# Two subtractions of the second layer's attention heads moved from the Vector engine to GpSimd

## The chip, the core and the metric

The kernel runs on one core of a Trainium2 chip. A core has five engines that run at the same time, each with its own instruction queue that it works through in order: TensorE (PE in the rows, its weight loads PEld), VectorE (DVE), ScalarE (ACT), GpSimd (POOL) and SyncE (SP), which here issues DMAs. An instruction that waits for a semaphore holds up everything behind it in its own queue, and nothing else. The metric is the device time of one execution in microseconds (us); lower is better.

## The reference, cut to what matters

Two sequences of 528 tokens (16 learned tokens and 512 given ones) go through two layers. The first is a bidirectional gated DeltaNet, the second is multi-head latent attention with 16 heads, each with 128 plain and 64 rotated ("rope") dimensions:

```python
q = (cq @ w_uq).reshape(B, L, MLA_HEADS, MLA_DQK)
kv = (ckv @ w_ukv).reshape(B, L, MLA_HEADS, MLA_NOPE + MLA_DV)
...
q = _rmsnorm(q, qk_q_g)
k = _rmsnorm(k, qk_k_g)
q = jnp.concatenate([q[..., :MLA_NOPE], _rope(q[..., MLA_NOPE:], cos, sin)], axis=-1)
k = jnp.concatenate([k[..., :MLA_NOPE], _rope(k[..., MLA_NOPE:], cos, sin)], axis=-1)
...
s = jnp.einsum('bqhd,bkhd->bhqk', qblk, k, preferred_element_type=jnp.float32) * scale
p = jax.nn.softmax(s, axis=-1)
return jnp.einsum('bhqk,bkhd->bqhd', p.astype(v.dtype), v)
...
y = o.reshape(B, L, MLA_V_WIDTH) * jax.nn.silu(z)
return y @ w_out
```

## The kernel before

Everything is fp32. A product a·b of two fp32 matrices is made of three TensorE passes: each operand is split into a high part (a cast to fp32r, by ScalarE) and a low part (the operand less its high part, a subtraction by `sub`, line 88), and `mm3` (lines 75 to 77) adds high·high, high·low and low·high. So nearly every tile costs one cast on ScalarE and one `sub` on VectorE or GpSimd. Weights are split by `weights`: the cast `wh` on ScalarE (line 219) and the low part `wl` on GpSimd (line 88); `last_wl` remembers the newest of these subtractions. As `sub` is a helper, all its instructions carry line 88, and the tile names tell them apart.

The second layer takes the heads in pairs, 8 for each sequence, 16 in all. While one pair's scores, softmax and outputs run (`pair_scores`, `pair_out`, eight query blocks), the generator `head` prepares the next pair: keys (`pair_k`), the rotated query (`pair_qrope`, whose half swap goes through DMA), its split (`pair_qsplit`), queries (`pair_q`), values (`pair_v`), normed keys (`pair_knorm`) and gates (`pair_z`). The order within an engine is settled when the program is built, by a scheduler with a timing model of its own. `behind` hands it an ordering edge: what is traced inside is queued behind the given instructions on the same engine.

The names that the steps below use:
- `acc` of line 964: the rotated query of both heads, the sum of two products that GpSimd made (lines 956, 957). VectorE adds them.
- `SQ` and `RL`: high and low part of the rotated query. Each is stacked with the other half (`SIDES`), so that one 128-row pass on TensorE does two of the three products. Per pair there are two `RL` subtractions of 64x512, both inputs in SBUF.
- `kst`: the rotated key, high part in one half of the partitions and low part in the other. Per pair two `kst` subtractions of 64x528, both inputs in SBUF.
- `mx`, `sm`, `P`: per block the negated row maximum (line 1089, read from PSUM; scaled in line 1090), the exponentials with their sum (line 1093, ScalarE), its reciprocal (line 1094) and the normed probabilities (line 1096, VectorE). TensorE transposes `P` (lines 1108 and 1110).
- `qL` (line 1012) and `hnL<-pj` (line 88): low parts of the queries and of the values, read by VectorE from the two projection buffers `pj` in PSUM. A buffer is free for the next projection when this has been done.
- `sqr` (line 1014 on GpSimd, then line 1015 on VectorE): sums of squares. The second needs the first.
- `kr` (line 1055): keys times their norm. `hnH<-tr`: low part of the transposed probabilities.

Of the kernel before, what the change touches and what calls it, by code (L numbers as in the profile page):

```python
# [23 lines left out]
class Trunk:  # L24
# [935 lines left out]
    def pair_qsplit(self, u):  # L960
        nc = self.nc
        V, A, G, PE = nc.vector, nc.scalar, nc.gpsimd, nc.tensor
        qg, sw = u["qg"], u["sw"]
        V.tensor_tensor(qg, qg, sw, op=ALU.add)
        RL = self.RL[u["hp"] % 2]
        SQ = [self.t("SQ%d" % j, [128, 512], F32R) for j in range(2)]
        for j, (o, nn) in enumerate(self.SIDES):
            A.copy(SQ[j][o], qg[o])
            nc.sync.dma_start(SQ[j][nn].bitcast(F32), SQ[j][o].bitcast(F32))
            self.sub(V, RL[j][o], qg[o], SQ[j][o])  # L970
        u.update(RL=RL, SQ=SQ)

    def pair_k(self, u):
# [76 lines left out]
    def pair_knorm(self, u, j):  # L1050
        nc = self.nc
        V, A, G, PE = nc.vector, nc.scalar, nc.gpsimd, nc.tensor
        c, kr, rs = u["c"], u["kr"], u["rs"]
        o, nn = self.SIDES[j]
        V.tensor_tensor(kr[:, j], kr[:, j], rs[:, j], op=ALU.mult)
        u["k"][j] = self.split("k", kr[:, j], [128, T])
        kp = self.t("acc", [128, T])
        G.tensor_tensor(kp, c["kpr"], rs[:, j], op=ALU.mult)
        kst = self.t("kst", [128, T], F32R)
        A.copy(kst, kp)  # L1060
        self.sub(V, kst[nn], kp[nn], kst[nn])
        u["kst"][j] = kst

    def pair_z(self, u, j):
# [64 lines left out]
    def run(self, rc, rs):  # L1129
# [76 lines left out]
        def head(u):  # L1206
            self.pair_k(u)
            yield
            self.pair_qrope(u)
            yield  # L1210
            with self.behind(self.last_sc, self.last_P):
                self.pair_qsplit(u)
            if u["hp"]:
                yield
            self.pair_q(u, 0)
            yield
            if u["hp"]:
                self.pair_v(u)
                with self.behind(self.last_sc, self.last_P, self.last_wl):
                    self.pair_knorm(u, 0)  # L1220
                yield
            self.pair_q(u, 1)
            with self.behind(self.last_sc, self.last_P, self.last_wl):
                if not u["hp"]:
                    self.pair_knorm(u, 0)
                self.pair_knorm(u, 1)
            yield
            self.pair_z(u, 0)
            yield
            if u["hp"] == 0:  # L1230
                self.pair_v(u)
                yield
# [13 lines left out]

        ends = [self.out_proj(y2[s], I["mla_w_out"][0], h1[s], hq[s], NM, 512, [tC, tA], finish(s)) for s in range(2)]
        fill = chain(self.l2_prep(0, h1[0], rsd[0], ctx[0]), head(units[0]))
        S = self.p("S", [128, 2, 512])
        pss[1] += [S[:, c, 0:264] for c in range(2)]  # L1250
# [10 lines left out]
        for i, u in enumerate(units):  # L1261
            edge = i % 8 == 7
            if not edge:
                fill = head(units[i + 1])
            else:
                fill = chain(self.l2_prep(1, h1[1], rsd[1], ctx[1]), head(units[8])) if i == 7 else ends[0]
            zat = 0 if i == 15 else 2
            for n in range(8):
                if n == zat and i != 7:
                    self.pair_z(u, 1)  # L1270
                for _ in range((2, 1, 2, 2, 2, 2, 2, 2)[n] if i == 7 else int(n > 0 or not edge)):
                    next(fill, None)
                if i == 6 and n == 7:
                    self.pair_z(units[7], 1)
                S, P = u["SP"]
                if n < 7:
                    self.pair_scores(u, (n + 1) // 4, (n + 1) % 4)
                elif i == 7:
                    drain(fill)
                    self.pair_scores(units[8], 0, 0)  # L1280
                elif i < 15:
                    self.pair_scores(units[i + 1], 0, 0)
                self.pair_out(u, n // 4, n % 4, S, P)
# [48 lines left out]
```

## Time and profile before

| | us |
|---|---|
| median of 3 runs | 2628.21 (2627.2 to 2632.5) |
| the profiled execution | 2632.01 |
| its span from first to last instruction | 2630.3 |

| engine | busy us | share of the span |
|---|---|---|
| TensorE | 2468.7 | 94% |
| VectorE | 1732.9 | 66% |
| ScalarE | 1408.4 | 54% |
| GpSimd | 1166.6 | 44% |

The profiled execution took 2632.01 us, 1.7 us more than its span, and lies 0.14% over the median. TensorE is the engine with the least idle time. The pairs of the second layer run from about 1500 to 2420 us of the span, and the lines that the diff touches run nowhere else. A row of the timeline is: start, duration, engine, line, operation, output and inputs, shapes, count; in brackets the idle time of the engine before it and what ended that wait. A row of a stretch is: the stretch, its length, busy us (and count) of PE, PEld, DVE, ACT and POOL, the granted TensorE clock (PEclk, 1.00 for the level of 2.4 GHz, 0.50 for that of 1.2 GHz), the busy share of the DMA engines, and GB/s.

### The profile page before, as it was taken

To read this page: it belongs to the slowest core of one execution; us is meant where nothing else is said; L and a number is where in the kernel's file an instruction comes from. 1 tells how busy PE (TensorE), PEld (TensorE's weight loads), DVE (VectorE), ACT (ScalarE), POOL (GpSimd) and SP (SyncE) were. 2 spreads that over 40 slices of the span, in tenths; PEclk is the share of its full clock that TensorE was granted. 3 is DMA by queue.
4 is the path that set the end of the run, shared out by engine and by line. 5 is a ranking of instruction groups with operands and counts; after the bars stand their busy time and mean duration, and the time that the engine had idled before them with its cause. 6 is when DMAs were issued, how large, how long until landed. Compare 5 with 4: busy or idle time off the path is not lost.

```text
span 2630.3 us, 52159 instructions
## 1 busy us (share of the span) xinstructions
PE 2468.7 (94%) x19083; PEld 2212.1 (84%) x19083; DVE 1732.9 (66%) x3915; ACT 1408.4 (54%) x3424; POOL 1166.6 (44%) x1157
## 2 busy tenths in 40 slices
PE   8889999998999999999989889998998989999999
PEld 7878888888888889888989878888887878888787
DVE  6987888777788867786454256667775567666421
ACT  5545655545455554545545365666656556665432
POOL 6544545432433323323445454555535544554343
PEclk9999999988999999999999999999999999999999
DMA  6544545442333354444465422233332223225575
GB/s 206 176 121 136 153 128 164 136 138 86 112 91 90 113 172 138 133 122 144 127 213 167 130 79 71 73 72 83 90 89 74 81 70 69 77 69 153 167 222 148
DMA packets 453216, 321.06 MB, mean 122 GB/s; under 512 B 134812, under 2 KB 364430, under 8 KB 452960
## 3 DMA queue, kind: packets, MB, share of 16 engines
q1 hardware_dynamic: 452960, 317.73, 41.9%
q8 instruction: 150, 2.46, 0.4%
q14 instruction: 106, 0.87, 0.1%
HBM read 216.02 MB, written 92.67 MB: 117 GB/s over the span
## 4 chain that ended last, share of the span: by engine, by line
PE 58%; DVE 20%; DMA 8%; ACT 6%; issue 4%; POOL 2%; SPq 2%; ACTq 0%; POOLq 0%; DVEq 0%
PE pj L75 12%; PE pj L76 12%; PE pj L77 12%; PE ch L692 2%; PE po L710 2%; DVE acc L374 2%; DVE RL L88 2%; DMA acc<-acc 2%; DVE Yt L504 1%; DVE kq L374 1%; PE ch L703 1%; DVE Y L506 1%; PE lv L552 1%; PE tr L1110 1%; DMA T<-Td 1%
## 5 line engine op out<-in xcount | busy, mean ns | idle before, releaser
L88 POOL TENSOR_TENSOR wl<-wraw,wh 128x512 fp32r<-128x512 f32 (+2 forms) x414 | 547.6, 1325 | 708.8 <-ACT wh L219 675.3
L75 PE MATMUL pj<-hnH,wh 128*128 128x264 f32 (+4 forms) x2080 | 632.8, 305 | 18.9 <-ACT wh L219 5.2
L77 PE MATMUL pj<-hnH,wl 128*128 128x264 f32 (+3 forms) x2080 | 627.6, 303 | 2.6 <-POOL wl L88 1.9
L76 PE MATMUL pj<-hnL,wh 128*128 128x264 f32 (+3 forms) x2080 | 625.2, 301 | 0.7 <-DVE hnL L784 0.6
L219 ACT CAST wh<-wraw 128x512 fp32r<-128x512 f32 (+2 forms) x414 | 248.2, 600 | 346.0 <-PE pj L76 195.8
L75 PEld LDWEIGHTS pj<-hnH,wh 128*128 128x128 f32 (+1 forms) x2080 | 398.9, 192 | 37.6 <-ACT wh L219 5.7
L77 PEld LDWEIGHTS pj<-hnH,wl 128*128 128x128 f32 (+1 forms) x2080 | 398.3, 192 | 17.8 <-POOL wl L88 3.3
L76 PEld LDWEIGHTS pj<-hnL,wh 128*128 128x128 f32 (+1 forms) x2080 | 399.0, 192 | 15.8 <-issue 2.5
L76 PE MATMUL pj<-h2L,wh 128*128 128x512 f32 (+1 forms) x544 | 205.5, 378 | 3.2 <-DVE h2L L88 3.1
L77 PE MATMUL pj<-h2H,wl 128*128 128x512 f32 (+1 forms) x544 | 205.8, 379 | 0.0
L75 PE MATMUL pj<-h2H,wh 128*128 128x512 f32 (+1 forms) x544 | 205.4, 379 | 0.3
L1089 DVE TENSOR_REDUCE mx<-S 128x1 f32<-128x528 f32 x128 | 89.9, 703 | 66.3 <-PE S L1086 65.5
L1093 ACT ACTIVATE P<-S,mx,qs 128x528 f32<-128x528 f32 x128 | 101.5, 793 | 46.6 <-DVE mx L1090 42.7
L76 PEld LDWEIGHTS pj<-h2L,wh 128*128 128x128 f32 x544 | 102.5, 188 | 22.4 <-DVE h2L L88 4.4
L732 POOL TENSOR_TENSOR oa<-oa,ot 128x256 f32<-128x256 f32 (+1 forms) x80 | 69.6, 870 | 114.5 <-DVE ot L730 101.2
L75 PEld LDWEIGHTS pj<-h2H,wh 128*128 128x128 f32 x544 | 102.3, 189 | 20.0 <-DVE cqL L916 0.6
L77 PEld LDWEIGHTS pj<-h2H,wl 128*128 128x128 f32 x544 | 102.7, 189 | 18.1
L374 DVE SCALAR_TENSOR_TENSOR acc<-raw,vec,acc 128x528 f32<-128x528 f32 x128 | 112.4, 881 | 6.7 <-ACT acc L372 5.7
L374 DVE SCALAR_TENSOR_TENSOR kq<-raw,vec,kq 128x528 f32<-128x528 f32 x128 | 105.7, 826 | 8.6 <-ACT kq L372 7.6
L793 DVE TENSOR_TENSOR raw<-raw,pj 128x512 f32<-128x512 f32 (+1 forms) x54 | 31.3, 580 | 120.9 <-PE pj L77 120.7
L1116 ACT CAST hnH<-tr 128x512 fp32r<-128x512 f32 x128 | 74.9, 585 | 61.5 <-PE tr L1110 59.6
L88 DVE TENSOR_TENSOR hnH<-tr,hnH 128x512 fp32r<-128x512 f32 x128 | 88.2, 689 | 19.6 <-ACT hnH L1116 16.1
(483 smaller groups left out, 6789.1 us busy)
## 6 DMA issues: line engine op xcount, KB each, us to landing
wraw<-in_gdn_w_in_dram SPq DMA_DIRECT2D x96, 256.0 KB
wc<-wh SPq DMA_DIRECT2D x96, 256.0 KB
wc<-wl SPq DMA_DIRECT2D x96, 256.0 KB
wh<-wc SPq DMA_DIRECT2D x96, 256.0 KB
wl<-wc SPq DMA_DIRECT2D x96, 256.0 KB
wraw<-in_mla_w_in_dram SPq DMA_DIRECT2D x88, 256.0 KB
wraw<-in_gdn_w_out_dram SPq DMA_DIRECT2D x64, 256.0 KB
wraw<-in_mla_w_out_dram SPq DMA_DIRECT2D x64, 256.0 KB
```

The costliest lines, as they stand in the source:

```text
L75: mm(out, ah, bh, start=first, stop=False)
L76: mm(out, ah, bl, start=False, stop=False)
L77: mm(out, al, bh, start=False, stop=last)
L88: return eng.tensor_tensor(out, a, hi, op=ALU.subtract)
L219: nc.scalar.copy(wh, raw)
L374: nc.vector.scalar_tensor_tensor(acc, raw[:, j:j + T], self.convw(j, u), acc, op0=ALU.mult, op1=ALU.add)
L692: PE.matmul(pc[:n, 0], kq[:, 0, sl], S[d], start=True, stop=True)
L710: PE.matmul(po[:n, 0], kq[:, 1, sl], S[d], start=True, stop=True)
L732: G.tensor_tensor(oa[:n, i], oa[:n, i], t, op=ALU.add)
L1089: V.tensor_reduce(mx, Sv, axis=AX.XY, op=ALU.max, negate=True)
L1093: self.last_P = A.activation(P, Sv, AF.Exp, bias=mx, scale=qs[j][:, qt:qt + 1], accum_out=sm)
L1116: A.copy(PTH[:, :, hc], pt)
```

## The change

`pair_qsplit` and `pair_knorm` make their subtractions with `G` (GpSimd) in place of `V` (VectorE). The ordering edges for `pair_qsplit` get `last_wl` added, a GpSimd instruction; the split of keys had that edge already. Nothing else is edited.

```diff
@@ pair_qsplit
         for j, (o, nn) in enumerate(self.SIDES):
             A.copy(SQ[j][o], qg[o])
             nc.sync.dma_start(SQ[j][nn].bitcast(F32), SQ[j][o].bitcast(F32))
-            self.sub(V, RL[j][o], qg[o], SQ[j][o])
+            self.sub(G, RL[j][o], qg[o], SQ[j][o])
@@ pair_knorm
         A.copy(kst, kp)
-        self.sub(V, kst[nn], kp[nn], kst[nn])
+        self.sub(G, kst[nn], kp[nn], kst[nn])
@@ run, head
-            with self.behind(self.last_sc, self.last_P):
+            with self.behind(self.last_sc, self.last_P, self.last_wl):
                 self.pair_qsplit(u)
```

The scheduler then orders the second layer anew. VectorE's queue in the third pair, before, from the sum of the rotated query (line 964) to the first normed probabilities behind it (line 1096):

```order
L964 TENSOR_TENSOR acc<-acc 128x512
L1125 SCALAR_TENSOR_TENSOR zs<-x,zs 128x256
L1089 TENSOR_REDUCE mx<-S 128x1
L88 TENSOR_TENSOR RL_19078<-acc,SQ_21907 64x512
L88 TENSOR_TENSOR RL_19079<-acc,SQ_21908 64x512
L1090 TENSOR_SCALAR mx<-mx,qs 128x1
L88 TENSOR_TENSOR hnH<-tr,hnH 128x4x128
L1094 RECIPROCAL sm<-sm 128x1
L1096 TENSOR_SCALAR P<-P,sm 128x528
```

The same stretch of VectorE's queue in the changed kernel:

```order
L964 TENSOR_TENSOR acc<-acc 128x512
L1125 SCALAR_TENSOR_TENSOR zs<-x,zs 128x256
L1089 TENSOR_REDUCE mx<-S 128x1
L1090 TENSOR_SCALAR mx<-mx,qs 128x1
L88 TENSOR_TENSOR hnH<-tr,hnH 128x4x128
L1094 RECIPROCAL sm<-sm 128x1
L1096 TENSOR_SCALAR P<-P,sm 128x528
```

The two RL rows that stood between the row maximum and the probabilities are gone from here, and the rest keeps its order. GpSimd's queue in the same pair, before, from the second product of the rotated query (line 957) to the second sum of squares (line 1014), with the two stacked key products of line 1058 in it:

```order
L957 TENSOR_TENSOR acc<-acc,rsn 128x512
L88 TENSOR_TENSOR wl<-wraw,wh 128x512
L1058 TENSOR_TENSOR acc<-kpr,rs_21817 128x528 x2
L88 TENSOR_TENSOR wl<-wraw,wh 128x512
L1014 TENSOR_TENSOR sqr<-sqr,raw 64x512
L88 TENSOR_TENSOR wl<-wraw,wh 128x512
L88 TENSOR_TENSOR wl<-wraw,wh 128x256
L1014 TENSOR_TENSOR sqr<-sqr,raw 64x512
```

And the same stretch of GpSimd's queue in the changed kernel:

```order
L957 TENSOR_TENSOR acc<-acc,rsn 128x512
L88 TENSOR_TENSOR wl<-wraw,wh 128x512
L1058 TENSOR_TENSOR acc<-kpr,rs_21817 128x528 x2
L88 TENSOR_TENSOR RL_19078<-acc,SQ_21907 64x512
L88 TENSOR_TENSOR RL_19079<-acc,SQ_21908 64x512
L88 TENSOR_TENSOR wl<-wraw,wh 128x512
L1014 TENSOR_TENSOR sqr<-sqr,raw 64x512
L88 TENSOR_TENSOR kst<-acc,kst 64x528
L88 TENSOR_TENSOR wl<-wraw,wh 128x512
L88 TENSOR_TENSOR wl<-wraw,wh 128x256
L1014 TENSOR_TENSOR sqr<-sqr,raw 64x512
```

Both RL now stand ahead of a weight split and of the first sum of squares, and the first kst ahead of two more weight splits; the second kst follows further on. A little later in the same pair, VectorE's queue before, from `kr` to the second low part of the values:

```order
L1055 TENSOR_TENSOR kr<-kr,rs_21817 128x528
L1015 TENSOR_TENSOR sqr<-sqr,raw 64x512
L88 TENSOR_TENSOR kst<-acc,kst 64x528
L88 TENSOR_TENSOR hnL<-pj,hnL 128x512
L88 TENSOR_TENSOR pst_19074<-S,pst_19074 16x128
L88 TENSOR_TENSOR hnH<-tr,hnH 128x4x128
L88 TENSOR_TENSOR hnL<-pj,hnL 128x512
```

And in the changed kernel:

```order
L1055 TENSOR_TENSOR kr<-kr,rs_21817 128x528
L1015 TENSOR_TENSOR sqr<-sqr,raw 64x512
L88 TENSOR_TENSOR hnH<-tr,hnH 128x4x128
L88 TENSOR_TENSOR hnL<-pj,hnL 128x512
L1089 TENSOR_REDUCE mx<-S 128x1
L88 TENSOR_TENSOR hnL<-pj,hnL 128x512
```

The kst is gone from here, and the values' low parts still stand behind the sum of line 1015, which needs GpSimd's line 1014.

## Rows read from the trace of the kernel before

**Rows 1.** Engines' busy time (count) in the pairs' stretch; PEclk, DMA share, GB/s.

```profile
1500.00:2420.00 920.00, 844.65 (x5460) 751.35 (x5460) 600.92 (x1153) 556.01 (x1237) 468.29 (x338) 0.98 0.31 81
```

**Rows 2.** Chain of work that ended last, same stretch: shares by engine and line.

```profile
by line: PE pj L75 11.3%; PE pj L76 10.5%; PE pj L77 10.1%; issue 4.9%; DVE RL L88 4.6%; DMA acc<-acc 4.5%; PE tr L1110 2.6%; PE x L76 2.2%; SPq L840 2.2%; DMA rkd<-rk 2.2%; PE x L77 2.0%; PE x L75 1.8%; PE S L1085 1.7%; PE S L75 1.7%; PE S
```

**Rows 3.** TensorE's waits, same stretch: us in total, times, longest us.

```profile
PE S L1108 <- DVE P L1096: 23.1, 12, 3.6
PE pj L75 <- DVE qL L1012: 17.9, 16, 5.4
```

**Rows 4.** VectorE's timeline in the third pair.

```profile
1616.34 0.69 DVE L1089 TENSOR_REDUCE mx<-S 128x1 f32<-128x528 f32 x1
1616.95 2.58 DVE L88 TENSOR_TENSOR RL<-acc,SQ 64x512 fp32r<-64x512 f32 x2
1619.57 0.21 DVE L1090 TENSOR_SCALAR mx<-mx,qs 128x1 f32<-128x1 f32 x1
...
1620.99 0.49 DVE L1096 TENSOR_SCALAR P<-P,sm 128x528 f32<-128x528 f32 x1
...
1624.78 0.69 DVE L1015 TENSOR_TENSOR sqr<-sqr,raw 64x512 f32<-64x512 f32 x1
...
1626.31 0.69 DVE L88 TENSOR_TENSOR hnL<-pj,hnL 128x512 fp32r<-128x512 f32 x1
```

**Rows 5.** TensorE's wait for these probabilities.

```profile
1621.63 0.37 PE L1108 MATMUL S<-ident,P 128*16 128x128 f32 x1 [3.60 <-DVE P L1096]
```

**Rows 6.** Groups in the pairs' stretch: count, busy us, mean ns, idle before.

```profile
L88 DVE TENSOR_TENSOR RL<-acc,SQ 64x512 fp32r<-64x512 f32 x32 | 42.8, 1337 | 4.9 <-ACT SQ L968 4.4
L88 DVE TENSOR_TENSOR kst<-acc,kst 64x528 fp32r<-64x528 f32 x32 | 26.3, 823 | 0.7
```

**Rows 7.** The same by tile, whole span: ns shortest/median/longest, first and last start.

```profile
L88 DVE TENSOR_TENSOR RL<-acc,SQ x32: 673/1670/1753, 1505.4 to 2378.2; 64x512 fp32r<-64x512 f32 x32
L1014 POOL TENSOR_TENSOR sqr<-sqr,raw x32: 1266/1290/1860, 1505.1 to 2394.8; 64x512 f32<-64x512 f32 x32
L1096 DVE TENSOR_SCALAR P<-P,sm x128: 478/495/1522, 1538.6 to 2465.2; 128x528 f32<-128x528 f32 x128
```

**Rows 8.** GpSimd's timeline in the third pair.

```profile
1615.49 3.50 POOL L1058 TENSOR_TENSOR acc<-kpr,rs 128x528 f32<-128x528 f32 x2
1621.35 1.27 POOL L88 TENSOR_TENSOR wl<-wraw,wh 128x512 fp32r<-128x512 f32 x1 [2.35 <-ACT wh L219]
1622.57 1.27 POOL L1014 TENSOR_TENSOR sqr<-sqr,raw 64x512 f32<-64x512 f32 x1
```

**Rows 9.** TensorE's first use of that pair's RL; kst one matmul ahead.

```profile
1648.36 0.28 PE L1086 MATMUL S<-kst,RL 128*128 128x264 f32 x1
```

**Rows 10.** A weight split on GpSimd and its first use on TensorE.

```profile
2158.17 1.28 POOL L88 TENSOR_TENSOR wl<-wraw,wh 128x512 fp32r<-128x512 f32 x1
...
2161.65 0.28 PE L76 MATMUL pj<-wl,ckvH 128*128 128x256 f32 x1
```

**Rows 11.** The first pair: RL on VectorE, and the wait on TensorE behind it.

```profile
1505.42 2.47 DVE L88 TENSOR_TENSOR RL<-acc,SQ 64x512 fp32r<-64x512 f32 x2
...
1508.74 0.59 PE L75 MATMUL pj<-hnH,wh 128*128 128x264 f32 x1 [2.80 <-DVE qL L1012]
```

**Rows 12.** Stretches as in rows 1: a wait, two falls of the clock.

```profile
1618.00:1621.30 3.30, 0.03 (x1) 0.00 (x0) 2.82 (x5) 1.42 (x4) 0.99 (x1) 1.00 0.32 75
1621.30:1628.10 6.80, 5.62 (x24) 4.57 (x25) 6.24 (x13) 5.43 (x13) 2.50 (x2) 0.50 0.07 19
...
2331.30:2334.70 3.40, 3.40 (x19) 3.40 (x17) 2.49 (x5) 0.58 (x1) 0.00 (x0) 0.50 0.02 5
```

**Rows 13.** The ninth pair: VectorE's kr, GpSimd beside it, TensorE's wait.

```profile
2006.70 4.67 DVE L1055 TENSOR_TENSOR kr<-kr,rs 128x528 f32<-128x528 f32 x1 [4.60 <-DMA rs<-rkd]
...
2007.00 2.58 POOL L1058 TENSOR_TENSOR acc<-kpr,rs 128x528 f32<-128x528 f32 x2
...
2013.79 0.58 PE L75 MATMUL pj<-wh,ckvH 128*128 128x256 f32 x1 [5.39 <-DVE qL L1012]
```

## The prediction

> **What bounds the kernel now.** I read the stretches first. In the 920 us in which the pairs run, TensorE is busy 845 us, VectorE 601 and GpSimd 468 [rows 1]. TensorE sets the pace, and no other engine is near its limit; only what TensorE waits for can be gained. The chain of waits for the same stretch says where that is: RL on VectorE is 4.6% of it, some 42 us [rows 2], almost all of the 42.8 us that the 32 RL take [rows 6]. An engine busy two thirds of the time stands in the way with one instruction.
>
> The list of TensorE's waits shows how. The largest two are for the normed probabilities P, 23.1 us in 12 waits, and for qL, 17.9 us in 16 [rows 3]. The timeline of the third pair shows why: behind the row maximum (ends 1617.03) come two RL, 2.58 us long, and only then the maximum's scaling (1619.57), which ScalarE needs for the exponentials [rows 4]. TensorE stands still for 3.60 us until P is there [rows 5]. The pattern repeats in most pairs: RL lands between a maximum and its P, or between the exponentials and P.
>
> RL is that slow because GpSimd is at work beside it. The shortest RL takes 673 ns, the median one 1670 ns, and GpSimd's 3.50 us of key products cover the third pair's two [rows 7, 8].
>
> **The change, part by part.**
>
> *Removed from VectorE.* 32 RL of 42.8 us and 32 kst of 26.3 us [rows 6]. Nothing of VectorE's total counts, as it isn't the limit. What counts is RL in front of P. A pair of RL is 42.8/16 = 2.67 us, and P comes earlier by about that. The 12 waits average 23.1/12 = 1.93 us, and the longest is 3.6 [rows 3]: most fall to zero, and a few of the longest keep up to 0.9 us. I allow 3 us for these: **20 us**.
>
> *qL.* It stands in the same queue behind P. Of its 17.9 us [rows 3], 5.4 belong to another cause [rows 13] and 2.8 to the first pair [rows 11]; 9.7 us in 14 waits are left. Below: nothing, as qL also needs ScalarE's two passes over the projection; above: all. I take half, **5 us**.
>
> *The first pair.* Its RL take 2.47 us right ahead of qL, and TensorE waits 2.80 us [rows 11]. Between 0 and 2.8, I take **2.5 us**.
>
> *The clock.* During the third pair's wait TensorE is busy 0.03 of 3.3 us; then the granted clock is 0.50, the 1.2 GHz level, for 6.8 us [rows 12]. The same happens behind such waits in six more places of the stretch, 3.4 us each, the last of them at 2331.3 [rows 12]. That is 6.8 + 6·3.4 = 27 us at half clock, a loss of 13.6 us if TensorE has work all along. Between 0 and 13.6, I take half, **7 us**, as the waits that remain may still bring the clock down.
>
> Together 20 + 5 + 2.5 + 7 = 34.5 us.
>
> *Added to GpSimd.* The trace has no such subtraction on GpSimd. The nearest row is its sum of the same 64x512 shape, 1266 to 1860 ns, median 1290 [rows 7]. 64 of them are 81 to 119 us. I take 1.29 us, so 83 us, as most of GpSimd's rows are near it: GpSimd goes from 468 to 551 of 920 us and stays off the limit. What stands behind the moved work on GpSimd is a weight split, then the first sum of squares, and, behind kst, two more splits. The splits have room: the tightest that I found ends 2.2 us ahead of its first use, at 2159.45 and 2161.65 [rows 10], and it stands ahead of RL in the queue. RL has nearly 29 us, 1619.53 to 1648.36, and the first kst, made ahead of 1626.31 and first used one matmul before RL, over 20 [rows 4, 9]. So both moves are hidden by the scores of the pair that runs meanwhile. Without that cover, each would cost 1.29 us less the 0.67 us it took on VectorE.
>
> *Where the stall goes.* VectorE reaches line 1015 earlier, but this sum needs GpSimd's line 1014, now behind two RL. In the third pair line 1014 ends at 1623.84 and line 1015 starts at 1624.78, 0.94 us later [rows 4, 8]. GpSimd idles 2.35 us ahead of the split there [rows 8], which takes most of the two RL's 2.6 us. So line 1014 ends about when it did, and VectorE, ahead by 2.6 us, will wait for it. Behind it hang the low parts of the values, which free TensorE's buffers; kst (0.7 us) no longer stands between. Between 0 and 34.5 us of what was won can be given back here. I take a third of a microsecond a pair, **5 us**, as TensorE has reordered scores to run meanwhile.
>
> *The shared port.* Every P, kr and sum with its inputs in SBUF can meet a GpSimd instruction: P takes 495 ns at the median and up to 1522 ns [rows 7], a microsecond more. GpSimd's share rises by 83/920, 9 points. By the code a pair has 15 of them on VectorE (8 P, 2 kr, 2 low parts of the keys, 3 sums), 240 in all. With half a GpSimd instruction, 0.65 us, for each meeting, that is 240·0.09·0.65 = 14 us of VectorE, of which a third may reach TensorE: between 0 and 14, I take **5 us**.
>
> Sum: 34.5 - 5 - 5 = 24.5 us. From the profiled execution's own 2632.0 us that gives 2607.5. The median of the runs is 3.8 us lower, so the forecast against it is 2628.2 - 24.5 = **2604 us**.
>
> **Row and rule on the port.** The longest P is 1044 ns over the shortest and the longest RL 1080 ns over its shortest [rows 7], each less than one 1290 ns instruction of GpSimd; but the ninth pair has a wait several instructions long [rows 13]. The Trainium skill, SBUF — State Buffer, section Summary: rules for kernel authors, says that where a VectorE instruction has two SBUF inputs and GpSimd reads SBUF, the second one to issue blocks until the first finishes. By that rule one meeting costs VectorE at most one GpSimd instruction, rival D below could not happen, and the sum would stay at 24.5 us with D's chance gone to A; the P and RL rows agree with it, the ninth pair's does not, and so D stays.
>
> **Rivals.**
>
> *A, the forecast.* Most waits for P go, some time is given back: 12 to 36 us, 2592 to 2616. Chance 0.5.
>
> *B, nothing given back.* P, qL, the first pair and all of the half clock: 23.1 + 9.7 + 2.8 + 13.6 = 49 us, 2579. For it speaks that the chain holds 42 us of RL [rows 2]; against it that qL also waits for ScalarE and that line 1015 waits for GpSimd. Chance 0.16, from 36 us on.
>
> *C, GpSimd takes back what VectorE frees.* Line 1015 ends no earlier than before, so the values' buffers and all behind them keep their times. The gain is then the part of TensorE's work that no longer hangs on them: the first pair and a few clock falls, 0 to 12 us, say 6: 2622. Chance 0.22; half of it is within 0.2%. The Trainium skill, Perfetto Trace Analysis, section Optimizing Scalar/DVE Operations, warns of this: moving work between the two "might not help", as they share a read port. The P and RL rows agree on the port; whether it eats the gain, no row of before shows.
>
> *D, slower: GpSimd's queue locks VectorE out.* In the ninth pair the first kr on VectorE takes 4.67 us beside back-to-back work on GpSimd, with two key products of 2.58 us passing by, and TensorE waits 5.39 us [rows 13]. The change makes such runs longer in each pair: two key products, two RL, a split and a sum, six in a row. If P or kr were locked out like this once in each of 15 pairs, each would cost 4.67 less the 0.67 of an undisturbed RL [rows 7], 4 us, some 3 of it on TensorE: 45 us against 34.5 gained, 2639. It decides from 34.5/15 = 2.3 us a pair on. Against it: this is the only wait of that length that I found on VectorE in the pairs; elsewhere one instruction passes. Chance 0.12.
>
> **How the numbers follow.** The likeliest case is A, 2604, by itself 2592 to 2616. The range 2580 to 2626 takes in A, nearly all of B and most of C, and leaves D's 0.12 and the ends of B and C out. Faster by over 0.2% (5.3 us, about what a measurement of this kernel can tell from no change): A, B and half of C, 0.5 + 0.16 + 0.11 = 0.77. Within 0.2%: half of C, 0.11. Slower: D, 0.12.
>
> **What the changed profile would show.** Right: TensorE's waits for P fall from 23.1 to under 6 us, RL leaves the chain of waits, fewer stretches are at PEclk 0.5, and TensorE's busy share in the pairs rises, with GpSimd at 540 to 560 us there. The GpSimd price is right if RL and kst take 1.27 to 1.4 us. C shows as VectorE idle ahead of line 1015 until GpSimd's line 1014, and as TensorE waiting for the values' low parts. D shows as P or kr of over 2.5 us. Wrong beyond these: a wait of TensorE for wl, or for kst at a first use.

## The result, and the profile after

The changed kernel takes 2603.89 us (median of 4 runs, 2597.6 to 2605.9), the kernel before 2627.7 us over 4 runs. The ratio is 0.9896, 95% interval 0.9875 to 0.9918: about 27 us or 1.0% faster, 24 us by the two medians. The forecast was 2604. The number was right; not all of the argument behind it was, and the rest of this text is about that.

The two profiled executions differ by more, 2632.01 against 2597.6 us. About 10 us of that arose before the pairs: the first sum of the rotated query (line 964) starts at 1500.77 us before and at 1490.89 after, although up to there the order of the compute engines is the same in both; in the other profiles of this text this sum starts between 1485.9 and 1508.8, so one profile can't settle some 10 us of a whole execution. The pairs' stretch is therefore 1490 to 2388 here, to be set beside [rows 1]:

```profile
1490.00:2388.00 898.00, 844.35 (x5462) 750.50 (x5462) 571.96 (x1091) 557.42 (x1237) 543.42 (x402) 0.98 0.31 83
```

The same matmuls (5462, 5460 before) take 898 us in place of 920, 22 us less. TensorE's idle time, length less busy time, falls from 75.4 to 53.7 us, and that is nearly all of it. GpSimd is at 543 us, as forecast. TensorE's longest waits there, beside [rows 3]:

```profile
PE x L76 <- DVE hnH L88: 12.5, 17, 2.6
PE pj L75 <- DVE qL L1012: 8.0, 6, 5.1
PE S L1108 <- DVE P L1096: 5.9, 6, 2.1
PE S L1108 <- DVE sm L1094: 4.2, 5, 0.9
...
PE pj L75 <- DVE hnL L88: 3.9, 4, 1.8
...
PE S L75 <- DVE pst L88: 2.3, 4, 0.8
PE x L75 <- ACT hnH L1116: 2.0, 1, 2.0
```

The wait for P is 5.9 us in place of 23.1; the five put down to `sm`, the reciprocal that follows, end just behind a P of 2.8 us and are waits for it. The largest wait is new: 12.5 us for `hnH`, the low part of the transposed probabilities, which stood at 2.1 before. `pst` is the split of the first 16 columns of the probabilities, transposed apart (line 1108). The same waits before, in the stretch of [rows 3]:

```profile
PE S L75 <- DVE pst L88: 11.0, 10, 1.4
PE x L75 <- ACT hnH L1116: 6.3, 8, 1.9
...
PE pj L75 <- DVE hnL L88: 2.8, 3, 1.3
PE x L76 <- DVE hnH L88: 2.1, 7, 0.3
```

The groups by tile, count, busy us and mean ns in the same stretch, and VectorE's wait for GpSimd's line 1014:

```profile
L1096 DVE TENSOR_SCALAR P<-P,sm 128x528 f32<-128x528 f32 x120 | 101.8, 848 | 2.9
L88 POOL TENSOR_TENSOR RL<-acc,SQ 64x512 fp32r<-64x512 f32 x32 | 44.9, 1403 | 1.3
L88 POOL TENSOR_TENSOR kst<-acc,kst 64x528 fp32r<-64x528 f32 x32 | 44.9, 1402 | 17.5 <-ACT kst L1060 16.6
L1055 DVE TENSOR_TENSOR kr<-kr,rs 128x528 f32<-128x528 f32 x31 | 34.5, 1116 | 4.2 <-DMA rs<-rkd 4.2
...
DVE sqr L1015 <- POOL sqr L1014: 13.3, 9, 1.9
```

Before, the 31 kr took 28.9 us; the P and that last wait stood at:

```profile
L1096 DVE TENSOR_SCALAR P<-P,sm 128x528 f32<-128x528 f32 x120 | 72.2, 601 | 2.7
...
DVE sqr L1015 <- POOL sqr L1014: 2.4, 4, 0.9
```

The fifth pair shows how the three meet. VectorE, then GpSimd, then TensorE:

```profile
1716.62 1.52 DVE L1096 TENSOR_SCALAR P<-P,sm 128x528 f32<-128x528 f32 x1
1718.06 1.81 DVE L1055 TENSOR_TENSOR kr<-kr,rs 128x528 f32<-128x528 f32 x1
1719.90 0.69 DVE L1015 TENSOR_TENSOR sqr<-sqr,raw 64x512 f32<-64x512 f32 x1
1720.51 0.68 DVE L88 TENSOR_TENSOR hnH<-tr,hnH 128x512 fp32r<-128x512 f32 x1
...
1715.29 1.29 POOL L88 TENSOR_TENSOR wl<-wraw,wh 128x512 fp32r<-128x512 f32 x1
1716.54 1.30 POOL L1014 TENSOR_TENSOR sqr<-sqr,raw 64x512 f32<-64x512 f32 x1
1717.91 1.39 POOL L88 TENSOR_TENSOR kst<-acc,kst 64x528 fp32r<-64x528 f32 x1
...
1721.24 0.38 PE L76 MATMUL x<-hnH,hnL 128*128 128x256 f32 x1 [2.57 <-DVE hnH L88]
```

P and kr each last past the end of the GpSimd instruction beside them, three and two and a half times as long as the shortest P and kr; `hnH` stands behind them and TensorE waits 2.57 us for it. Where RL used to stand in the way, GpSimd's work now does.

Last, where in the program the time was won. Five pair periods of the first sequence and the same five of the second, from the second (tenth) pair's first matmul with RL to the seventh's (fifteenth's), before and then after:

```profile
1590.84:1865.20 274.36, 252.95 (x1659) 225.80 (x1658) 184.93 (x361) 168.47 (x384) 141.09 (x101) 0.98 0.30 74
2080.61:2356.94 276.33, 252.55 (x1660) 225.76 (x1658) 184.83 (x361) 168.51 (x384) 140.20 (x101) 0.98 0.29 73
```

```profile
1580.09:1849.70 269.61, 253.53 (x1658) 226.89 (x1657) 171.16 (x342) 168.25 (x382) 161.84 (x121) 0.97 0.28 74
2068.30:2325.45 257.15, 247.06 (x1653) 220.41 (x1651) 170.31 (x341) 167.55 (x378) 161.27 (x120) 1.00 0.30 78
```

The first sequence gains 4.8 us in five pairs, the second 19.2, although the same instructions moved in both. The two differ in their order: in the second sequence the scheduler found another one for TensorE and VectorE, the same in pairs eleven to fourteen, in which VectorE makes the values' first low part ahead of line 1015. In the kernel before it stands so in every second pair, and both sequences have one order. That led to the experiments on order.

### The profile page after: what moved, and what is told of

Same layout as the page of the kernel before. It is cut to its first block, busy times and chain, and to the rows that moved or that the text cites. A ratio compares the mean times of both kernels' runs of the same rounds, so it can differ in the third digit from the quotient of the medians.

```text
span 2595.9 us, 52222 instructions
## 1 busy us (share of the span) xinstructions
PE 2462.8 (95%) x19083; PEld 2208.1 (85%) x19083; DVE 1698.0 (65%) x3851; ACT 1410.1 (54%) x3424; POOL 1241.9 (48%) x1221
## 4 chain that ended last, share of the span: by engine, by line
PE 39%; DVE 7%; DMA 4%; ACT 4%; POOL 2%; issue 2%; SPq 1%; ACTq 0%; DVEq 0%; POOLq 0%
PE pj L75 9%; PE pj L76 9%; PE pj L77 9%; PE tr L1110 1%; DVE P L1096 1%; PE x L76 1%; DMA rkd<-rk 1%; PE x L77 1%; DVE hnH L88 1%; PE x L75 1%; PE S L75 1%; PE S L1085 1%; PE S L76 1%; PE S L1086 1%; DMA acc<-acc 1%
## 5 line engine op out<-in xcount | busy, mean ns | idle before, releaser
L88 POOL TENSOR_TENSOR wl<-wraw,wh 128x512 fp32r<-128x512 f32 (+2 forms) x414 | 540.7, 1308 | 583.6 <-ACT wh L219 544.1
L374 DVE SCALAR_TENSOR_TENSOR kq<-raw,vec,kq 128x528 f32<-128x528 f32 x128 | 107.1, 838 | 10.5 <-ACT kq L372 9.5
L1096 DVE TENSOR_SCALAR P<-P,sm 128x528 f32<-128x528 f32 x128 | 105.9, 828 | 3.1
```

The lines of the kernel that those rows point to most:

```text
L88: return eng.tensor_tensor(out, a, hi, op=ALU.subtract)
L374: nc.vector.scalar_tensor_tensor(acc, raw[:, j:j + T], self.convw(j, u), acc, op0=ALU.mult, op1=ALU.add)
L1096: self.last_sc = V.tensor_scalar(P, P, sm, None, op0=ALU.mult)
```

## Experiments

All ratios are against the kernel before on the same chip. To compare runs I turn them into us with its median, about 2626 us. Each run also has its mean granted clock. As the two levels are 1.00 and 0.50, a mean of 0.97 over 2626 us is 2·0.03·2626 = 158 us at the lower one, and half of that is what full speed would have saved if TensorE had work all along.

**The parts, each with the order that the scheduler then gives.** The changed kernel again:

> The changed kernel once more, to be compared with the parts. All theories: 24 us under the kernel before, 2601 to 2607 us against its 2628; in its trace again seven P of 2.8 us on VectorE, each beside the second kst and a weight split on GpSimd.

0.9904 (0.9881 to 0.9927), 2602.37 us. Its trace has the seven P of 2.8 us again, and its ten periods take 268.64 and 255.41 us.

Only RL moved:

```diff
-        self.sub(G, kst[nn], kp[nn], kst[nn])
+        self.sub(V, kst[nn], kp[nn], kst[nn])
```

> Only RL goes to GpSimd, kst stays on VectorE. Theory 1 (the gain comes from RL's leaving the place in front of P, and kst on GpSimd costs, as P waits behind two GpSimd instructions in seven pairs, 0.85 us of TensorE each): 6 to 10 us faster than the changed kernel, 30 to 34 us under the kernel before. Theory 2 (RL's leaving gives the gain, kst is free either way): the same as the changed kernel, 24 us under before, give or take 4. Theory 3 (half of the gain comes from kst's leaving the place in front of the values' low parts): 10 to 15 us under before.

1.0036 (1.0021 to 1.005), slower than before, against all three theories. In its trace the wait for P falls to 12.1 us and that for `hnH` rises to 27.4, in 25 waits. One of them, in the thirteenth pair, VectorE and then TensorE:

```profile
2231.60 1.55 DVE L1096 TENSOR_SCALAR P<-P,sm 128x528 f32<-128x528 f32 x1
2233.07 0.69 DVE L1055 TENSOR_TENSOR kr<-kr,rs 128x528 f32<-128x528 f32 x1
2233.80 0.70 DVE L88 TENSOR_TENSOR kst<-acc,kst 64x528 fp32r<-64x528 f32 x1
2234.54 0.69 DVE L1015 TENSOR_TENSOR sqr<-sqr,raw 64x512 f32<-64x512 f32 x1
...
2235.88 0.38 PE L76 MATMUL x<-hnH,hnL 128*128 128x256 f32 x1 [2.19 <-DVE hnH L88]
```

kst on VectorE now stands with kr and line 1015 in front of `hnH`.

Only kst moved, from the kernel before, so without the edge to `last_wl`:

```diff
-        self.sub(V, kst[nn], kp[nn], kst[nn])
+        self.sub(G, kst[nn], kp[nn], kst[nn])
```

> Only kst goes to GpSimd, RL stays on VectorE. Theory 1: no faster than the kernel before, 0 to 8 us slower. Theory 2: the same as before within 4 us. Theory 3: 10 to 15 us under before.

1.0103 (1.0085 to 1.012), 27 us slower, worse than any theory had it. TensorE waits for P 29.4 us in its pairs and for qL 18.7, with RL still in front of both. Most of the 27 us is the clock: its mean is 0.960 in these six runs and 0.968 in the 15 of the kernel before, 46 us more at the lower level.

RL made by no engine:

> RL is made by no engine (the low part of the rotated query stays zero, that part of the scores is left out), kst stays on VectorE: what RL's leaving VectorE is worth when GpSimd gets nothing in return. By the sum on record 34.5 us of waits go and only a little comes back: 30 to 35 us under before. If the shared port costs little, RL only on GpSimd comes within 3 us of this run; if it costs what VectorE's longer P and kr say (30 us of VectorE, a third of it on TensorE), this run is some 10 us faster than RL only on GpSimd.

```diff
-            self.sub(V, RL[j][o], qg[o], SQ[j][o])
+            pass
```

0.9944 (0.9928 to 0.996): 15 us, not 30 to 35. Taking RL from VectorE at no price at all gives less than the whole change does. And it isn't idle time of TensorE: from the first pair's first matmul with RL to the last one's that is 68.0 us, against 70.3 before. By the means it is the clock, 0.974 in six runs against 0.968 in 15, 31 us less at the lower level. TensorE's and GpSimd's order in the inner pairs is the same as with RL alone on GpSimd, but VectorE's isn't: line 1015 stands ahead of kr and kst here and behind them there; nor is the edge to `last_wl` in this kernel. So the 24 us between the two, 1.0036 less 0.9944, are the price of RL on GpSimd and of that place together, and don't measure the 10 us of give-back and port in the sum on record alone. The theory that RL in front of P carries the gain by itself fell here, in the order that the scheduler gave.

**Move and order apart.** The next kernels hold every engine to a list of its instructions, by edges within the engine alone. `ORDER` is the list of the kernel before for the first of them and that of the changed kernel for the second, with the 64 subtractions put in where the expectations say:

```diff
+    ids = {i.name: i for i in tc.nc.cur_bb.bb.instructions}
+    for names in ORDER.values():
+        row = [ids[n] for n in names]
+        for a, b in zip(row, row[1:]):
+            tc.add_manual_dep(b, a.name, NO_SYNC, reason="order")
```

> RL and kst on GpSimd as in the changed kernel, but all five engines are held to the order of the kernel before (an edge from each instruction to the one before it on its engine); the 64 moved subtractions stand on GpSimd behind the instruction that they follow in the changed kernel. The move theory (taking RL from VectorE gives the 24 us, the new order is incidental): 18 to 28 us under before. The order theory (the move gives little by itself, the new order in the second sequence's pairs gives the gain): within 8 us of before. If GpSimd's work costs more than VectorE's queue gives, as RL alone and kst alone were slower than before: 5 to 20 us over before.

1.0000 (0.998 to 1.0021). With the old order, and these places in GpSimd's queue, the move is worth nothing, give or take 5 us.

> RL and kst on VectorE as in the kernel before, but all five engines are held to the order of the changed kernel; RL stands two places behind the sum of the rotated query, the first kst behind the first kr, the second in front of the P behind the norms. The move theory: within 5 us of before. The order theory: 15 to 28 us under before, like the changed kernel. If both are needed: between, or slower than before, as RL then stands in front of a P for which this order leaves no room.

0.9993 (0.9968 to 1.0018). With RL and kst on VectorE, at these places, the new order is worth nothing clear of noise either. Both together are the changed kernel, 0.9896. Neither theory stands by itself. One set of places was run for each; other places for the 64 subtractions in the old order, on GpSimd above all, were not.

What eats the gain in the old order is in its trace: TensorE's waits, VectorE's wait for line 1014, and the thirteenth pair, VectorE and TensorE, with GpSimd's row last.

```profile
PE pj L75 <- DVE qL L1012: 13.9, 9, 5.2
PE S L1108 <- DVE P L1096: 12.1, 8, 2.5
PE pj L75 <- DVE hnL L88: 10.1, 8, 2.5
DVE sqr L1015 <- POOL sqr L1014: 27.1, 15, 3.1
...
2217.13 0.69 DVE L1015 TENSOR_TENSOR sqr<-sqr,raw 64x512 f32<-64x512 f32 x1 [1.76 <-POOL sqr L1014]
2217.74 0.68 DVE L88 TENSOR_TENSOR hnL<-pj,hnL 128x512 fp32r<-128x512 f32 x1
2218.47 0.29 PE L75 MATMUL pj<-wh,ckvH 128*16 128x256 f32 x1 [0.75 <-DVE hnL L88]
2215.81 1.29 POOL L1014 TENSOR_TENSOR sqr<-sqr,raw 64x512 f32<-64x512 f32 x1
```

Part of it is rival C to the letter: line 1014 stands behind two RL and a split, line 1015 waits 1.76 us for it, `hnL` stands behind line 1015 and TensorE waits for `hnL`, 10.1 us in all against 2.8. And half of the wait for P stays, 12.1 us, because P is held by GpSimd: in front of each of the eight waits P takes 0.95 to 2.70 us, in place of 0.49. The longest in the twelfth pair:

```profile
2181.47 2.88 DVE L1096 TENSOR_SCALAR P<-P,sm 128x528 f32<-128x528 f32 x1
2184.79 2.70 DVE L1096 TENSOR_SCALAR P<-P,sm 128x528 f32<-128x528 f32 x1
...
2181.48 1.33 POOL L88 TENSOR_TENSOR kst<-acc,kst 64x528 fp32r<-64x528 f32 x1 [1.60 <-PE pj L77]
2182.77 1.29 POOL L88 TENSOR_TENSOR wl<-wraw,wh 128x512 fp32r<-128x512 f32 x1
```

In this profile the rest is the clock. From the first pair's first matmul with RL to the last one's, before and then here:

```profile
1533.69:2416.59 882.90, 812.62 (x5254) 722.04 (x5253) 582.15 (x1127) 536.87 (x1205) 448.70 (x323) 0.98 0.30 79
1523.51:2406.60 883.09, 819.62 (x5254) 726.99 (x5253) 573.30 (x1067) 536.76 (x1205) 519.65 (x384) 0.97 0.30 79
```

TensorE's idle time falls from 70.3 to 63.5 us, 6.8 in all, and its busy time for the same 5254 matmuls rises by 7.0. The granted clock is at the 1.2 GHz level for 41.0 us of the one and for 54.6 of the other, 6.8 us of work at half speed. But that is one execution of each. The two profiles of the changed kernel differ as much in the same stretch, 34.1 and 20.5 us, and the mean granted clock is 0.970 in the twelve runs with the old order and 0.969 in the 25 of the kernel before. So that the clock takes back what the stalls gave isn't shown; the 6.8 us of idle time are little more than what the ratio's interval leaves open.

**The second sequence's order in both.** If that order is what makes the move pay, it should pay in the first sequence too. `ORDER` is the changed kernel's, and in turns two to five of the pair loop that of turns ten to thirteen:

> The changed kernel, with its second to fifth turns of the pair loop (first sequence) held to the order that the tenth to thirteenth have. In the changed kernel's trace the pairs of the first sequence take 53.5 us each and those of the second 51.2. The order theory: 8 to 12 us faster than the changed kernel, 32 to 36 us under before. The move theory: as the changed kernel, since nothing is moved between engines.

0.9878 (0.9849 to 0.9907), 32 us under before. In its trace the five periods of the first sequence take 260.33 us, of the second 255.52, against 269.61 and 257.15 above. The following four runs have this order, and only the engine of RL and kst differs, `V` or `G` in the two lines of the change; in the last of the four a few instructions of TensorE and ScalarE stand elsewhere too, in one pair each.

> The second sequence's order in both sequences, as in the run at 2590 us, with RL and kst all on VectorE (RL two places behind the sum of the rotated query, in front of a P; the first kst behind the first kr, the second in front of the P behind the norms). If move and order are both needed: 2612 to 2625 us, 22 to 35 us slower than with both on GpSimd. If this order alone is good: within 8 us of that run.

0.9979 (0.9961 to 0.9996).

> The same order, RL on GpSimd, both kst on VectorE. If RL in front of P is what costs, as the forecast had it: the greater part of the gain is there, 2590 to 2605 us. If kst is worth as much, 2605 to 2615; the second kst alone was worth 16 us in this order.

0.9945 (0.9926 to 0.9964).

> The same order, both kst on GpSimd, RL on VectorE. By the forecast (RL carries the gain): 2608 to 2625 us, near the run with all on VectorE. If kst carries it: 2590 to 2605.

0.9945 (0.9925 to 0.9965), 2611 us: in the range for RL, but RL alone gave no more than this.

> As the run with the second sequence's order in both, with the second kst of each pair back on VectorE, behind the maximum's scaling. In the changed kernel that kst and a weight split hold a P for 2.8 us in seven pairs, and TensorE stands still for 0.85 us and then 0.34. If that lock-out costs what these waits say: 10 to 16 us faster than with the second kst on GpSimd. If VectorE's place is worth as much: within 4 us of it. If kst in front of P costs as RL did: slower by 5 us or more.

0.9928 (0.9903 to 0.9952), 13 us slower than with the second kst on GpSimd: the third case.

| in this order, on GpSimd | ratio | us under before |
|---|---|---|
| nothing | 0.9979 | 5 |
| RL | 0.9945 | 14 |
| both kst | 0.9945 | 14 |
| RL and the first kst | 0.9928 | 19 |
| RL and both kst | 0.9878 | 32 |

RL and kst are worth about the same, some 9 us each alone and some 18 on top of the other. Each interval is some 5 us to either side, so a difference of two rows has 7 to 9; that the second is worth more than the first isn't shown. Little of it is the clock, whose mean is 0.9747 with nothing moved and 0.9755 with both, against 0.9691 in the kernel before; that part came with the order. Why kst is dear on VectorE is seen with nothing moved, in the thirteenth pair: VectorE, then TensorE.

```profile
2200.03 2.51 DVE L88 TENSOR_TENSOR RL<-acc,SQ 64x512 fp32r<-64x512 f32 x2
2204.22 0.49 DVE L1096 TENSOR_SCALAR P<-P,sm 128x528 f32<-128x528 f32 x1
2226.78 0.70 DVE L88 TENSOR_TENSOR kst<-acc,kst 64x528 fp32r<-64x528 f32 x1 [1.47 <-ACT kst L1060]
2227.41 0.68 DVE L88 TENSOR_TENSOR hnH<-tr,hnH 128x512 fp32r<-128x512 f32 x1
...
2204.86 0.27 PE L1108 MATMUL S<-ident,P 128*16 128x128 f32 x1 [1.48 <-ACT hnH L1116]
2228.14 0.39 PE L76 MATMUL x<-hnH,hnL 128*128 128x256 f32 x1 [0.57 <-DVE hnH L88]
```

RL holds up P and with it TensorE's transposes, 1.48 us (the view names ScalarE's `hnH`, but P's end at 2204.71 is what comes last). kst waits 1.47 us for ScalarE's cast at the head of VectorE's queue, and `hnH` behind it costs TensorE 0.57 us. So the price of kst there is that wait more than its 0.7 us. The sums say so too: with RL on VectorE, both kst on GpSimd take the waits for `hnH` from 10.5 to 3.4 us and those for `pst` from 17.2 to 6.7, and add 8.5 for a P held by the second kst (put down to `sm`): 9 us less. But I put kst there; in the kernel before it stood where it hardly waited, 0.7 us in all [rows 6]. What it cost in that kernel these runs don't show.

With RL and kst on GpSimd the fourteenth pair has two waits left, P held by the second kst and a split, and line 1015 behind line 1014:

```profile
2257.61 2.79 DVE L1096 TENSOR_SCALAR P<-P,sm 128x528 f32<-128x528 f32 x1
2240.11 0.69 DVE L1015 TENSOR_TENSOR sqr<-sqr,raw 64x512 f32<-64x512 f32 x1 [1.74 <-POOL sqr L1014]
...
2260.55 0.27 PE L1108 MATMUL S<-ident,P 128*16 128x128 f32 x1 [0.82 <-DVE sm L1094]
2241.46 0.39 PE L76 MATMUL x<-hnH,hnL 128*128 128x256 f32 x1 [0.77 <-DVE hnH L88]
```

**Two places in GpSimd's queue.** With all on GpSimd again, `ORDER` is changed in each inner pair:

```diff
 RL RL
+sqr (line 1014)
 wl
-sqr (line 1014)
...
-kst (the second)
 wl sqH wl sqH rk
+kst (the second)
```

> The same order with all on GpSimd, and two places changed in GpSimd's queue: the first sum of squares (line 1014) directly behind the two RL, ahead of a weight split, and the second kst four instructions later, behind the power for the keys' norms, where no P stands. In the trace at 2585 us VectorE waits 1.7 us a pair for line 1014 and TensorE 0.77 us behind it, and P takes 2.8 us beside the second kst with 0.85 us of TensorE behind it. If these two waits are what is left: 8 to 18 us faster than without the two changes, 2572 to 2582 us. If the waits only move to the next instruction: within 4 us of it, 2586 to 2594. If the split that now comes later holds TensorE: slower.

0.9837 (0.981 to 0.9863), 43 us under before and the fastest kernel here, though its median, 2585, lies just over the 2572 to 2582 expected. The five periods of each sequence take 256.95 and 253.99 us.

From the first pair's first matmul with RL to the last one's the profile is 840.16 us long against 849.08 without the two changes, 9 us; the ratios say 11, but they come from two chips and their intervals overlap. VectorE's wait for line 1014 falls from 20.3 to 6.2 us in that stretch, and the waits put down to `sm`, 8.5 us, are gone; `pst` rises from 3.4 to 7.7. So the two waits together had a price, and part of it moved on; neither place was changed alone.

## Why the prediction was right, and where it wasn't

*What bounds the kernel.* Right: TensorE sets the pace, and what was gained in this profile is idle time of TensorE, 21.7 of 22 us. The second profile of the changed kernel, from the first pair's first matmul with RL to the last one's, is 25.6 us shorter than the kernel before: 17.6 us of idle time, and 8.1 us less busy time for the same matmuls.

*RL in front of P (20 us).* Off: the wait for P went from 23.1 to 5.9 + 4.2 us, 13 gained. The step "P comes earlier by about that" failed in its silent assumption that VectorE and TensorE keep their order and P its length. With the order kept, 11 us of the wait for P go, `hnL` takes back 7.3, and the move alone measures 1.0000.

*qL and the first pair (7.5).* The wait for qL went from 17.9 to 8.0 us, 9.9. The cause isn't shown to be RL, as in the old order only 4 us of it went.

*The clock (7).* Missed in these two profiles, not in the runs. PEclk is at the 1.2 GHz level for 41.0 us of the stretch, in nine places, against 44.4 us in ten before, summed from the granted clock in the trace: 1.7 us at half speed. Falls came back behind other waits: at 1722.60 to 1726.00 it is 0.50, just behind the 2.57 us wait for `hnH` above. But over the runs the mean granted clock is 0.9689 in 57 of the kernel before and 0.9733 in ten of the changed kernel, 163 and 139 us at the lower level: 24 us less, 12 us of work at half speed, give or take 5. Up to the pairs both kernels have one order, so this should be the pairs' doing. The term is then there, and nearer its upper bound of 13.6 than 7. It need not be RL's: with the second sequence's order in both, the pairs have 20.5 us at that level with all on GpSimd and 17.1 with nothing moved, against 41.0 in the same stretch before. There the order keeps the clock up.

*The price on GpSimd.* Nearly right: 1.40 us each, so 90 us in place of 83. No weight split keeps TensorE waiting for as much as 0.5 us.

*The give-back at line 1015 (5) and the port (5).* Both mechanisms are there, and on VectorE both are larger than worked out: line 1015 waits 13.3 us, not 2.4, and P and kr take 29.6 and 5.6 us more in the stretch, 35 us where 14 were worked out. On TensorE they come to about what was put down, 11.5 us for 10, but by another way: the wait for the values' low parts, which the sum named, rises by 1.1 us only, and that for `hnH`, which it didn't name, by 10.4.

*kst, priced at nothing.* This is the other weak step. The text counted kst as VectorE time that isn't the limit. In the second sequence's order, at the place that I gave it, it is worth about as much as RL; what it was worth in the kernel before isn't shown. The waits for `pst` and for `hnH`'s cast fell by 8.7 and 4.3 us, and the sum had no term for them. That they fell by kst isn't shown either, as the order changed too.

Put together: 13 for P, 9.9 for qL, 1.7 for the clock and 13 unpriced, less 11.5 given back, make 26 us by the rows of this profile, of which the stretch shows 22. There P and the clock were 12 us too large, and the 13 us without a term made up for them. That the total held is in good part luck.

*Rivals.* C, GpSimd takes back what VectorE frees, is what happens in the old order. D's sign was there too, seven P of 2.8 us; the kr of 4.79 us is no sign of it, as the kernel before has one of 4.67 in the same pair [rows 13]. Its price was not, as TensorE waits at most 0.9 us for such a P here, not 3; with the old order it waited 2.5 us for the one of 2.70. The Trainium skill, SBUF — State Buffer, section Summary: rules for kernel authors, would have a meeting cost one GpSimd instruction at most; these P waited for two, and the measurement decides.

*What stays open.* Which difference in the order lets the move pay wasn't isolated; the values' low part ahead of line 1015 is one candidate, but the kernel before has it in every second pair. Whether other places in GpSimd's queue would let the move pay in the old order is open as well: in the second sequence's order two such places were worth some 10 us. Why the scheduler finds that order in the second sequence alone is a matter of its own model. How much of the changed kernel's gain the port took can't be told apart from the queue, since no run has one without the other.

## What to carry to other kernels

Where a scheduler settles the order, a change of engine is two changes. Measure the move in the old order and the new order without the move before a reason is given; here each alone, at the places tried, was worth nothing and both 1%. A forecast that hits the total proves none of its terms: check each against its own row. One profile can't settle a term of a few us: two profiles of one kernel had 34.1 and 20.5 us at the lower clock, and the mean clock of all runs said more than either. And price an instruction by what it waits for at the head of its queue and by what stands behind it, not by its length.

## What the runs showed of the hardware

A VectorE instruction with its input in SBUF can be held by two GpSimd instructions that follow each other without a gap. With the second sequence's order, P started at 2257.61 beside a kst and a split and took 2.79 us, against 0.49 undisturbed. At 2184.79 of the run with the old order another took 2.70 beside a sum and a split. In the ninth pair of the changed kernel a kr took 4.79 us while three GpSimd instructions began and ended beside it. Where GpSimd is idle beside it, as in the kernel with the two changed places, the same P of another pair takes 0.48 us: it starts at 2191.84, in a gap of 1.72 us in GpSimd's queue that ends at 2192.32.

The granted clock differs from one execution of a kernel to the next. In the stretch of the pairs the two profiles of the changed kernel have 34.1 and 20.5 us at the 1.2 GHz level, with every engine's order the same.
